# Norm weights spread by a TensorE product, small first loads on ScalarE's queue, the second token half projected first, and norms by power, VectorE and transposes

## The chip, the cores and the metric

The kernel runs on one core of a Trainium2 chip. The metric is the device time of one launch in microseconds (us), lower is better. The kernel before has a median of 930.0 us in three runs (924.01 to 930.1 us).

## What is computed

One layer of a hybrid encoder over 528 tokens (16 learned ones and 512 of the input) of width 1024, everything in float32. A root-mean-square norm gives `u`; one wide projection of `u` gives the inputs of a latent attention branch (16 heads) and of a state-space branch (SSD, four groups of eight heads, two directions); both branches are gated, projected, added to the input, and normed once more.

```python
def rmsnorm(x, w):
    y = x * lax.rsqrt(jnp.mean(x * x, axis=-1, keepdims=True) + NORM_EPS)
    return y * w

u = rmsnorm(h, norm_w)                    # h: 528 x 1024
proj = u @ w_in                           # 1024 x 8928
q_lat, kv_lat, k_rope, g_attn, z, xbc, dt_raw, merge = jnp.split(proj, offsets, axis=-1)
y_a = mla_branch(q_lat, kv_lat, k_rope, ...)            # norms q_lat and kv_lat first
y_a = (y_a * jax.nn.silu(g_attn)) @ w_attn_proj
y_s = ssd_branch(z, xbc, dt_raw, ...)                   # conv over tokens, scan, norm per group
y_s = y_s @ w_ssd_proj
gates = jax.nn.sigmoid(merge)
h = h + (gates[0] * y_a + gates[1] * y_s) @ w_out
h = rmsnorm(h, final_norm_w)
```

Seven norms lie in the way: that of `h` at the start, one for each SSD group, one for `q_lat`, one for `kv_lat` (and the last one, which the change leaves alone).

## The kernel before

Everything that feeds a product is held transposed, features on partitions and tokens along the row. A float32 product is made from three products of a reduced type: each factor is split into a high part (rounded, by ScalarE) and a low part (the rest, by VectorE), and `proj` (line 522) adds high by high, high by low and low by high, in that order. With 1024 input features these are 3 times 8 matmuls of a 128-column weight tile on 512 tokens, or on two token halves of 264 (270 where a convolution follows). The weights `wr` come by DMA in pieces of 512 KB (two buffers), are split to `wh` and `wl` (three buffers each), and are used up by TensorE.

**The start.** The token blocks `xt` (four of 128 tokens, and 16 learned ones) and the norm weights `nw` (copied to all 128 partitions by the DMA itself, two halves of 512) are loaded on SyncE's queue in the order of `LOADS` (line 44). For each block `u_stats` (564) sums the squares on ScalarE and raises the mean to the power -1/2 on GpSimd (`rr`); `u_scale` (574) multiplies by `rr` and `nw` on VectorE (`xw`); `u_split` (583) transposes on TensorE (`tr`, against the identity `ident` in the tile `cst`, itself a DMA from `masks`), and splits into `uh` and `ul`. The blocks go in the order of `UORDER`. Then come `dt_stage` (655), the projection for the time steps and the rope key, and the six projections with convolutions of group 0 (`in_units`, 768; the tiles `B`, `C`, `x`), and after them the four gates `z`.

**The norms inside.** `rms_rows` (981) squares the tiles (`sq`), adds them on VectorE, sums over partitions by a product with ones (`ssq`), takes mean and epsilon on VectorE, the power on GpSimd (`rc`), and spreads the row over all partitions by a float32 product with the identity (`rb`, line 1008). VectorE then multiplies by `rb`.

**Attention.** For each head: scores (`sc`), the maximum on VectorE, the exponential on ScalarE (`p`), transposes of the probabilities (`pt`), their split (`pT`), the product with the values (`o`, `y`). GpSimd multiplies `y` by the gate (line 1275, `YG`) and the query's rope part by the sine (line 1117, `RPE`): 8 and 4 instructions.

**What sets the order.** All code is recorded first (`_Recorder`, 94; `drive`, 1451, picks which unit of work goes on), with an estimated cost for each instruction (`_Eng`, 266; `_Queue`, 338). `order` (166) then places the instructions one after another by these costs, and that fixes each engine's instruction order. On the chip each engine runs its own list in order and waits where an operand is missing. Because one line emits every instruction, all rows carry line 263 and are told apart by their tiles.

Of the kernel before, what the change touches and what calls it, by code (L numbers as in the profile page):

```python
# [16 lines left out]
P = 128  # L17
D = 1024
NM = 16
# [22 lines left out]
NRM, YG, YL, RPE, PEL = "VVVA", "G", "V", "VGV", "V"  # L42
UORDER = (0, 1, 2, 4, 3)
LOADS = "0a1bi243"
UPOOL = ()
# [48 lines left out]
class _Recorder:  # L94
# [71 lines left out]
    def order(self):  # L166
# [41 lines left out]
        while len(out) < len(ops):  # L208
# [20 lines left out]
            if o.eng == "PE" and o.four != four:  # L229
                four, more = o.four, self.SWITCH  # L230
            elif o.both:
                lock = t + o.occ
            elif o.eng == "POOL":
                port = t + o.occ - 50.0
# [31 lines left out]
class _Eng:  # L266
# [3 lines left out]
    def __getattr__(self, op):  # L270
        fn = getattr(self.eng, op)

        def call(*args, **kw):
# [31 lines left out]
            if self.name == "PE":  # L305
                if op == "transpose":
                    occ, lat = 109.0, 271.0
                elif lhs.dtype == F32R:
                    occ = max(109.0, {270: 126.0, 264: 122.0, 256: 118.0}.get(n, 0.4476 * n + 3))
                    lat = occ + 165  # L310
                    if lhs.shape[0] == 64:
                        occ, lat = 427.0, 493.0
                else:
                    occ = max(109.0, 2 * 0.838 * n)
                    occ = occ if n > 1 else 223.0
                    occ = occ / 2 if cols == 64 else occ
                    lat = occ + 165
            elif self.name == "ACT":
                occ = (50 if psum else 99) + 0.834 * k + 95 * ptr + (60 if "accum_out" in kw else 0)
# [18 lines left out]
class _Queue:  # L338
    def __init__(self, plan, rec, eng):
        self.plan, self.rec, self.eng = plan, rec, eng  # L340

    def dma_start(self, out, in_, after=0.0):
        n = 4 * out.shape[0]
        for d in out.shape[1:]:
            n *= d
        self.plan.op("DMA", 2000.0 + n / 330.0, out, [in_], after)
        wide = "cum_rows" in in_.name
        self.rec.add("SP", self.eng.dma_start, (out, in_), {}, 420.0, (1.3 if wide else 1.1) * n / 262.0, [out], [in_],
                     extra=1000.0 if wide else 0.0)
# [3 lines left out]
def hybrid_block_kernel(ctx, tc, a, out):  # L353
# [70 lines left out]
    S = _Queue(plan, rec, nc.sync)  # L424
# [97 lines left out]
    def proj(w, src, cols, M=P, tag="m", width=HALF):  # L522
# [6 lines left out]
        seq = [(hi, 0, k) for k in range(n)] + [(hi, 1, k) for k in range(n)] + [(lo, 0, k) for k in range(n)]  # L529
        for h, s in enumerate(parts):  # L530
            o = ps[:M, :cols.stop - cols.start] if tag == "m" else ps[:M, h, :width]
            for i, (x, y, k) in enumerate(seq):
                mm(o, x[:, k, :], src[k][y][:, s], start=(i == 0), stop=(i == len(seq) - 1))
                mid[0] = h < len(parts) - 1 or i < len(seq) - 1
# [29 lines left out]
    def u_stats(c):  # L564
# [5 lines left out]
        for j in range(2):  # L570
            if (c, j) in UPOOL:
                tt(G, xw[c][j], xt[c][:, j * 512:(j + 1) * 512], nw[j], ALU.mult)

    def u_scale(c):
        R = rows(c)
        for j in range(2):
            if (c, j) in UPOOL:
                A.activation(xw[c][j], xw[c][j], AF.Copy, scale=rr[c][:, 0:1])
            else:
                V.scalar_tensor_tensor(xw[c][j][:R], xt[c][:R, j * 512:(j + 1) * 512], rr[c][:R, 0:1], nw[j][:R],  # L580
                                       op0=ALU.mult, op1=ALU.mult)
# [10 lines left out]

    steps = UORDER
    for i in range(len(steps) + 2):
        if i < len(steps):
            u_stats(steps[i])
        if 1 <= i <= len(steps):
            u_scale(steps[i - 1])
        if i >= 2:
            u_split(steps[i - 2])  # L600
# [380 lines left out]
    def rms_rows(tiles, n, dim):  # L981
        blocks = [(j, min(P, n - j)) for j in range(0, n, P)]
        acc = None
        for t in tiles:
# [5 lines left out]
            else:  # L990
                tt(V, acc, acc, q, ALU.add)
# [15 lines left out]
        for i, (j, R) in enumerate(blocks):  # L1007
            mm(pb[:, j:j + R], rc[:R, i:i + 1].broadcast_to([R, P]), ident[:R, :R])
# [474 lines left out]

    main(setup)
    fill([mark(dt_stage, "dt")])
    in_fill(0)
    for g in range(NG):
# [11 lines left out]
        fill(z_units(g))  # L1499
# [78 lines left out]
```

## Time and profile before

| | us |
|---|---|
| median of three runs | 930.0 |
| the profiled execution, its own time | 927.54 |
| its span, first to last instruction | 925.8 |
| TensorE busy in it | 880.9 |
| VectorE busy | 702.2 |
| ScalarE busy | 545.5 |
| GpSimd busy | 38.7 |

In the profile PE is TensorE, PEld its weight loads, DVE is VectorE, ACT ScalarE, POOL GpSimd, SP SyncE (SPq its queue). A row of the timeline has start, duration, engine, operation, tiles and, in brackets, how long the engine sat idle before it and what ended that. The granted clock of TensorE is 1.0 for 2.4 GHz and 0.5 for 1.2 GHz.

### The profile page before, as it was taken

How to read it: one execution, taken by the hardware profiler on the slowest of the kernel's cores; microseconds unless marked ns; L12 is line 12 of the kernel's file. 1: busy time of each engine (PE TensorE's matmuls, PEld its weight loads, DVE VectorE, ACT ScalarE, POOL GpSimd, SP SyncE). 2: the span in 40 equal slices, each digit the busy share in tenths (PEclk: the TensorE clock that was granted, in tenths of full speed). 3: DMA queues.
4: the chain of work that ended last, by engine and by line, in shares of the span. 5: the costliest groups of instructions: out<-in, count | busy, mean ns of one | idle time of the engine just before them, and what ended most of it. 6: DMA issues, size and time to landing. Idle time of an engine off the chain costs nothing.

```text
span 925.8 us, 13360 instructions
## 1 busy us (share of the span) xinstructions
PE 880.9 (95%) x5005; PEld 728.5 (79%) x5005; DVE 702.2 (76%) x1233; ACT 545.5 (59%) x1152; POOL 38.7 (4%) x32
## 2 busy tenths in 40 slices
PE   4999999999999999999999999999999999999997
PEld 4997878776899768866787788887778777888875
DVE  6797699978699599987857855979989897334364
ACT  5379468866656366875334455767777785432232
POOL 1000000100000000010002000101000000000000
PEclk8999999999999999999999999999999999999999
DMA  6474227325432333542221342212111011442222
GB/s 194 114 188 114 69 69 204 92 77 139 125 97 89 90 86 105 130 136 70 64 74 46 103 114 70 61 33 49 38 41 40 10 29 46 137 137 91 91 69 91
DMA packets 127237, 83.83 MB, mean 91 GB/s; under 512 B 26384, under 2 KB 114101, under 8 KB 127173
## 3 DMA queue, kind: packets, MB, share of 16 engines
q1 hardware_dynamic: 127173, 82.99, 32.4%
q8 instruction: 39, 0.64, 0.3%
q14 instruction: 25, 0.20, 0.1%
HBM read 80.74 MB, written 2.23 MB: 90 GB/s over the span
## 4 chain that ended last, share of the span: by engine, by line
PE 71%; DVE 18%; ACT 5%; issue 2%; POOL 2%; DMA 1%; SPq 0%; POOLq 0%; ACTq 0%; DVEq 0%
PE pj L263 50%; PE wo L263 4%; DVE x L263 4%; PE sc L263 3%; PE st L263 2%; PE yo L263 2%; PE o L263 2%; PE pt L263 2%; DVE wl L263 2%; PE tr L263 2%; DVE w L263 1%; POOL rc L263 1%; PE yd L263 1%; DVE mx L263 1%; DVE pT L263 1%
## 5 line engine op out<-in xcount | busy, mean ns | idle before, releaser
L263 DVE TENSOR_TENSOR wl<-wr,wh 128x1024 fp32r<-128x1024 f32 (+1 forms) x102 | 124.8, 1224 | 77.9 <-ACT wh L263 58.0
L263 PE MATMUL pj<-uh,wh 128*128 128x270 f32 (+3 forms) x776 | 160.6, 347 | 7.0 <-DVE yo L263 4.2
L263 ACT CAST wh<-wr 128x1024 fp32r<-128x1024 f32 (+1 forms) x102 | 106.3, 1045 | 101.3 <-PE pj L263 71.7
L263 PE MATMUL pj<-ul,wh 128*128 128x270 f32 (+3 forms) x776 | 156.1, 338 | 0.0
L263 PE MATMUL pj<-uh,wl 128*128 128x270 f32 (+3 forms) x776 | 149.8, 335 | 0.0
L263 PEld LDWEIGHTS pj<-uh,wh 128*128 128x128 f32 (+1 forms) x776 | 121.4, 190 | 28.2 <-DVE yo L263 5.7
L263 PEld LDWEIGHTS pj<-uh,wl 128*128 128x128 f32 (+1 forms) x776 | 122.4, 189 | 15.0
L263 PEld LDWEIGHTS pj<-ul,wh 128*128 128x128 f32 (+1 forms) x776 | 121.1, 189 | 13.2 <-issue 0.3
L263 ACT ACTIVATE ar<-ar,nacs 128x128 f32<-128x128 f32 x256 | 80.9, 392 | 12.9 <-DMA ar<-cum_rows 8.7
L263 PE MATMUL sc<-kst,qst 96*128 96x264 f32 (+1 forms) x384 | 66.6, 299 | 3.2 <-ACT p L263 1.7
L263 PEld LDWEIGHTS sc<-kst,qst 96*128 96x128 f32 (+1 forms) x384 | 53.4, 189 | 7.7 <-ACT p L263 3.5
L263 PE MATMUL pt<-cst,p 128*128 128x128 f32 (+1 forms) x320 | 52.1, 273 | 6.1 <-DVE pT L263 5.3
L263 ACT ACTIVATE p<-sc,mx 128x528 f32<-128x528 f32 x64 | 45.0, 704 | 19.7 <-DVE mx L263 18.1
L263 DVE TENSOR_TENSOR pT<-pt,pT 128x512 fp32r<-128x512 f32 x64 | 43.6, 684 | 12.5 <-ACT pT L263 12.3
L263 PEld LDWEIGHTS pt<-cst,p 128*128 128x128 f32 (+1 forms) x320 | 37.4, 130 | 16.9 <-DVE pT L263 4.7
L263 ACT CAST pT<-pt 128x512 fp32r<-128x512 f32 x64 | 37.1, 585 | 21.2 <-PE pt L263 20.8
L263 DVE SCALAR_TENSOR_TENSOR x<-pj,chv,x 128x528 f32<-128x528 f32 x64 | 48.6, 762 | 0.8 <-ACT x L263 0.6
L263 DVE TENSOR_REDUCE mx<-sc 128x1 f32<-128x528 f32 x64 | 44.5, 696 | 4.5 <-PE sc L263 4.3
L263 PE MATMUL o<-pT,v 128*128 128x512 f32 x128 | 46.6, 417 | 1.4 <-ACT pT L263 1.2
L263 ACT ACTIVATE w<-cbm,dt_t 128x128 f32<-128x128 f32 x128 | 40.3, 392 | 4.8 <-DVE cbm L263 4.8
L263 PE MATMUL pj<-nh,wh 128*128 128x512 f32 x128 | 39.8, 435 | 1.5 <-ACT nh L263 1.5
L263 DVE SCALAR_TENSOR_TENSOR w<-cbm,dt_t,w 128x128 f32<-128x128 f32 x128 | 38.4, 348 | 0.0
(221 smaller groups left out, 1493.0 us busy)
## 6 DMA issues: line engine op xcount, KB each, us to landing
wr<-in_w_in SPq DMA_DIRECT2D x69, 512.0 KB, 3.8
ar<-cum_rows SPq DMA_DIRECT2D x32, 512.0 KB, 5.6
wr<-in_w_ssd_proj SPq DMA_DIRECT2D x16, 512.0 KB, 3.4
wr<-in_w_attn_proj SPq DMA_DIRECT2D x8, 512.0 KB, 3.5
wr<-in_w_out SPq DMA_DIRECT2D x8, 512.0 KB, 3.6
ws<-in_w_uq SPq DMA_DIRECT2D x36, 64.0 KB, 3.0
xt<-in_x SPq DMA_DIRECT2D x4, 512.0 KB, 6.4
fin<-in_x SPq DMA_DIRECT2D x4, 512.0 KB, 3.9
```

Of the source, the lines that this page charges most:

```text
L263: o.fn(*o.args, **o.kw)
```

## The change

A line of "..." stands for unchanged code, or for cost estimates of the planner that nothing below speaks of.

```diff
-NRM, YG, YL, RPE, PEL = "VVVA", "G", "V", "VGV", "V"
-UORDER = (0, 1, 2, 4, 3)
-LOADS = "0a1bi243"
-UPOOL = ()
+NRM, YG, YL, RPE, PEL = "VVVA", "V", "V", "VVV", "V"
+LOADS = "3abi2104"
...
             elif o.eng == "POOL":
-                port = t + o.occ - 50.0
+                port = t + o.occ + 60.0
...
-    S = _Queue(plan, rec, nc.sync)
+    S, Q = _Queue(plan, rec, nc.sync), _Queue(plan, rec, nc.scalar, "ACT")
...
         if step == "i":
-            S.dma_start(ident, a["masks"][:, 0, :])
+            Q.dma_start(ident, a["masks"][:, 0, :])
         elif step in "ab":
             j = "ab".index(step)
-            w = slot([P, 512], name="nw")
-            S.dma_start(w, a["norm_w"][0, j * 512:(j + 1) * 512].partition_broadcast(P))
+            w = slot([1, 512], name="nw")
+            Q.dma_start(w, a["norm_w"][:, j * 512:(j + 1) * 512])
             nw.append(w)
         else:
             c = int(step)
             t = xt[c] = big([P, D], name="xt")
             if c == NC:
-                S.dma_start(t[:NM], a["meta_tokens"])
+                Q.dma_start(t[:NM], a["meta_tokens"])
...
+    nwb = [psm([P, 512], name="nwb") for _ in range(2)]
+    for j in range(2):
+        mm(nwb[j], ones[:1, :], nw[j][:1, :])
...
-        seq = [(hi, 0, k) for k in range(n)] + [(hi, 1, k) for k in range(n)] + [(lo, 0, k) for k in range(n)]
-        for h, s in enumerate(parts):
+        seq = [(hi, 0, k) for k in range(n)] + [(lo, 0, k) for k in range(n)] + [(hi, 1, k) for k in range(n)]
+        for h, s in list(enumerate(parts))[::-1]:
...
-                V.scalar_tensor_tensor(xw[c][j][:R], xt[c][:R, j * 512:(j + 1) * 512], rr[c][:R, 0:1], nw[j][:R],
-                                       op0=ALU.mult, op1=ALU.mult)
+            V.scalar_tensor_tensor(xw[c][j][:R], xt[c][:R, j * 512:(j + 1) * 512], rr[c][:R, 0:1], nwb[j][:R],
+                                   op0=ALU.mult, op1=ALU.mult)
...
-                tt(V, acc, acc, q, ALU.add)
+                V.scalar_tensor_tensor(acc, acc, dim * EPS / P if t is tiles[1] else 0.0, q, op0=ALU.add, op1=ALU.add)
...
-                V.tensor_scalar(rc[:rows, cs], pc[:rows, cs], 1.0 / dim, EPS, op0=ALU.mult, op1=ALU.add)
+                A.copy(rc[:rows, cs], pc[:rows, cs])
                 tt(G, rc[:rows, cs], rc[:rows, cs], mhalf[:rows, cs], ALU.pow)
+                V.tensor_scalar(rc[:rows, cs], rc[:rows, cs], dim ** 0.5, None, op0=ALU.mult)
...
-            mm(pb[:, j:j + R], rc[:R, i:i + 1].broadcast_to([R, P]), ident[:R, :R])
+            T.transpose(pb[:, j:j + R], rc[:R, i:i + 1].broadcast_to([R, P]), ident[:R, :R])
...
+    for step, c in ((u_stats, 3), (u_stats, 2), (u_scale, 3), (u_stats, 1), (u_scale, 2), (u_split, 3), (u_scale, 1), (u_split, 2),
+                    (u_split, 1)):
+        step(c)
+    begin([mark(dt_stage, "dt")])
+    for step in (u_stats, u_scale, u_split):
+        step(0)
+    first = [mark(u, ("in", 0, i)) for i, u in enumerate(in_units(0))]
+    begin(first[:1])
+    for step in (u_stats, u_scale, u_split):
+        step(NC)
     main(setup)
-    fill([mark(dt_stage, "dt")])
-    in_fill(0)
+    zs = z_units(0)
+    for k in "1a2345bcd":
+        fill([first[int(k)] if k.isdigit() else zs["abcd".index(k)]], lambda: True)
```

The norm weights now arrive as one row each and are spread to 128 partitions by a product with ones into PSUM (`nwb`), which VectorE reads in place of `nw`. They, the identity and the learned tokens are issued by ScalarE. The projection of a tile in two halves begins with the second token half, which needs blocks 3, 2 and 1 only, and inside a half the low weights come before the low activations. The gates `z` of group 0 are mixed into its convolutions.

On TensorE, the first rows of the program. `tr` are transposes of `xw`, `pj` products of the projections; before:

```order
L263 MATMUL tr_119<-cst,xw_103 128x128 x4
L263 MATMUL tr_120<-cst,xw_104 128x128 x4
L263 MATMUL tr_123<-cst,xw_105 128x128 x4
L263 MATMUL tr_124<-cst,xw_106 128x128 x4
L263 MATMUL tr_127<-cst,xw_107 128x128 x4
L263 MATMUL tr_128<-cst,xw_108 128x128 x4
L263 MATMUL tr_129<-cst,xw_111 128x16 x4
L263 MATMUL tr_130<-cst,xw_112 128x16 x4
L263 MATMUL pj_157<-uh,wh_148 96x264 x4
L263 MATMUL pj_159<-uh,wh_151 128x270
```

and of the changed kernel:

```order
L261 MATMUL nwb_102<-nw_96,ones 128x512
L261 MATMUL nwb_103<-nw_97,ones 128x512
L261 MATMUL tr_133<-cst,xw_111 128x128 x4
L261 MATMUL tr_134<-cst,xw_112 128x128 x4
L261 MATMUL tr_135<-cst,xw_109 128x128 x4
L261 MATMUL tr_136<-cst,xw_110 128x128 x4
L261 MATMUL tr_137<-cst,xw_107 128x128 x4
L261 MATMUL tr_138<-cst,xw_108 128x128 x4
L261 MATMUL pj_158<-uh,wh_140 96x264 x4
L261 MATMUL pj_161<-uh,wh_147 128x270 x3
L261 MATMUL tr_144<-cst,xw_105 128x128 x4
```

Two spreading products stand first, and the transposes of the learned tokens (two groups of 16 columns) have moved behind the first projection products.

On VectorE, around the first group's norm: `rc` is the row of 1/rms, `wl`, `w` and `ar` are instructions with two SBUF operands that belong to other work. Before:

```order
L263 TENSOR_TENSOR wl_348<-wr_337,wh_347 128x1024
L263 TENSOR_SCALAR rc_341<-ssq_340 128x4
L263 TENSOR_TENSOR wl_351<-wr_342,wh_350 128x1024
L263 TENSOR_TENSOR w_241_345<-w_241_345,ar_344 128x512
L263 TENSOR_TENSOR ar_412<-ar_412 128x512
L263 TENSOR_TENSOR ar_421<-ar_421 128x512
L263 TENSOR_TENSOR ar_433<-ar_433 128x512
L263 SCALAR_TENSOR_TENSOR x_67_171<-x_67_171,chv,rb_343 128x512 x4
```

and changed:

```order
L261 TENSOR_TENSOR wl_348<-wr_340,wh_347 128x1024
L261 SCALAR_TENSOR_TENSOR w_248_352<-cbm_304,dt_t,w_248_352 128x128 x3
L261 SCALAR_TENSOR_TENSOR z_343<-z_343,pj_337 128x512
L261 TENSOR_TENSOR xw_358<-tr_353,wst 128x512
L261 SCALAR_TENSOR_TENSOR w_248_352<-cbm_304,dt_t,w_248_352 128x128
L261 TENSOR_SCALAR rc_350<-rc_350 128x4
L261 TENSOR_TENSOR ar_429<-ar_429 128x512
L261 TENSOR_TENSOR w_248_352<-w_248_352,ar_351 128x512
L261 TENSOR_TENSOR ar_442<-ar_442 128x512
L261 TENSOR_TENSOR ar_446<-ar_446 128x512
L261 SCALAR_TENSOR_TENSOR x_81_185<-x_81_185,chv,rb_357 128x512 x4
```

Before, VectorE's `rc` stood ahead of GpSimd's power, with a run of five such instructions right behind it; now `rc` is the scaling that waits for the power, and four of that run stand behind it. On TensorE 12 products of 512 columns stand between `ssq` and `rb` before, and 4 transposes and 12 such products after.

On VectorE in attention, where the gate product enters. `o` is a head's output, `z` the gate. Before:

```order
L263 TENSOR_TENSOR y_1042<-o_1069,y_1042 64x512
L263 RECIPROCAL sm_1105<-sm_1105 128x1
L263 COPY qst_815<-qpl_1081 32x512
L263 TENSOR_TENSOR pT_1104<-pt_1103,pT_1104 128x512
L263 TENSOR_TENSOR pT_1112<-pt_1111,pT_1112 128x512
```

and changed:

```order
L261 COPY qst_811<-qpl_1083 32x512
L261 TENSOR_REDUCE mx_1108<-sc_1115 128x1
L261 RECIPROCAL sm_1107<-sm_1107 128x1
L261 TENSOR_SCALAR p_1112<-p_1112,sm_1107 128x528
L261 TENSOR_TENSOR y_1044<-o_1071,y_1044 64x512
L261 TENSOR_TENSOR pT_1106<-pt_1105,pT_1106 128x512
L261 TENSOR_TENSOR y_1044<-y_1044,z_1035 128x512
L261 TENSOR_TENSOR pT_1114<-pt_1113,pT_1114 128x512
```

The gate product is VectorE's own instruction between two splits of `pT`, and the copy to `qst` has moved ahead of the sum into `y`.

## Rows read from the trace of the kernel before

**Rows 1.** The page, part 1: busy us and share of the span.
```profile
PE 880.9 (95%) x5005; PEld 728.5 (79%) x5005; DVE 702.2 (76%) x1233; ACT 545.5 (59%) x1152; POOL 38.7 (4%) x32
```

**Rows 2.** Waits of TensorE: total us, times, longest.
```profile
PE rb L263 <- POOL rc L263: 3.7, 2, 1.9
...
PE pj L263 <- DVE B L263: 1.3, 1, 1.3
```

**Rows 3.** The timeline of the start, all engines.
```profile
1.17 0.43 SPq L263 DMA_DIRECT2D nw<-in_norm_w  x1
...
3.06 0.74 SPq L263 DMA_DIRECT2D xt<-in_x  x1
...
3.98 1.06 ACT L263 ACTIVATE junk<-xt 128x1024 f32<-128x1024 f32 x1 [1.97 <-DMA xt<-in_x]
...
6.75 0.75 DVE L263 SCALAR_TENSOR_TENSOR xw<-xt,rr,nw 128x512 f32<-128x512 f32 x1 [1.44 <-DMA nw<-in_norm_w]
8.15 1.06 ACT L263 ACTIVATE junk<-xt 128x1024 f32<-128x1024 f32 x1 [3.02 <-DMA xt<-in_x]
...
9.47 0.75 DVE L263 SCALAR_TENSOR_TENSOR xw<-xt,rr,nw 128x512 f32<-128x512 f32 x1 [1.97 <-DMA nw<-in_norm_w]
...
10.96 1.42 DVE L263 SCALAR_TENSOR_TENSOR xw<-xt,rr,nw 128x512 f32<-128x512 f32 x2 [0.67 <-POOL rr L263]
...
18.60 1.86 PE L263 MATMUL pj<-uh,wh 128*96 128x264 f32 x7
```

**Rows 4.** Stretches of the start: busy us per engine, granted clock, DMA share, GB/s.
```profile
10.00:20.00 10.00, 7.34 (x38) 6.13 (x38) 9.05 (x19) 8.24 (x17) 3.02 (x4) 0.84 0.81 205
20.00:25.00 5.00, 5.00 (x30) 5.00 (x29) 4.29 (x9) 1.17 (x2) 0.00 (x0) 0.64 0.41 107
```

**Rows 5.** The chain that ended last, in order of time: start, us, one piece.
```profile
2.59 7.07 DMA cst<-in_masks
```

**Rows 6.** DMA issues: size and us from issue to landing.
```profile
dtb<-in_dt_bias SPq DMA_DIRECT2D x1, 0.2 KB, 2.3
```

**Rows 7.** Groups by shape: count, busy us, mean ns of one row, idle before.
```profile
L263 PE MATMUL st<-xw,bt 128*128 128x512 f32 x48 | 24.9, 601 | 0.0
...
L263 PE MATMUL tr<-cst,x 128*128 128x128 f32 x64 | 9.8, 276 | 0.0
...
L263 PE MATMUL rb<-cst,rc 128*128 128x128 f32 x48 | 6.9, 288 | 3.8 <-POOL rc L263 3.7
...
L263 DVE TENSOR_TENSOR x<-x,z 128x512 f32<-128x512 f32 x16 | 10.1, 685 | 0.0
...
L263 ACT COPY bm<-tr 16x128 f32<-16x128 f32 x4 | 1.0, 247 | 0.0
```

**Rows 8.** The timeline around two of the inner norms.
```profile
173.40 4.24 POOL L263 TENSOR_TENSOR rc<-rc,mhalf 128x4 f32<-128x4 f32 x1 [155.04 <-DVE rc L263]
...
173.83 2.00 PE L263 MATMUL pj<-uh,wl 128*128 128x512 f32 x8
...
174.88 1.89 DVE L263 TENSOR_TENSOR ar<-ar 128x512 f32<-128x512 f32 x3
```

**Rows 9.** GpSimd's timeline, the second group's norm.
```profile
274.60 1.01 POOL L263 TENSOR_TENSOR rc<-rc,mhalf 128x4 f32<-128x4 f32 x1 [96.95 <-DVE rc L263]
```

**Rows 10.** Attention: the timeline at one gate product, and the wait at another.
```profile
660.64 1.28 POOL L263 TENSOR_TENSOR y<-y,z 128x512 f32<-128x512 f32 x1 [14.51 <-DVE y L263]
660.73 1.48 DVE L263 CAST qst<-qpl 32x512 fp32r<-32x512 f32 x1
...
662.99 0.44 PE L263 MATMUL pt<-cst,p 128*128 128x128 f32 x2 [1.57 <-DVE pT L263]
...
721.84 0.44 PE L263 MATMUL pt<-cst,p 128*128 128x128 f32 x2 [1.55 <-DVE pT L263]
```

**Rows 11.** The copies to `qst` on VectorE: ns min/median/max, first and last start.
```profile
L263 DVE CAST qst<-qpl x13: 416/419/1482, 572.7 to 755.3; 32x512 fp32r<-32x512 f32 x13
```

**Rows 12.** One stretch of four heads, columns as in rows 4.
```profile
660.64:719.50 58.86, 54.93 (x343) 46.82 (x342) 51.51 (x107) 43.85 (x96) 3.87 (x3) 1.00 0.15 35
```

More of the change, by code (lines that the diff above doesn't have):

```diff
@@ L318, in call @@
             elif self.name == "ACT":
-                occ = (50 if psum else 99) + 0.834 * k + 95 * ptr + (60 if "accum_out" in kw else 0)
+                occ = (50 if psum else 99) + 0.834 * k + 95 * ptr + (13 if "accum_out" in kw else 0)
                 lat = occ + 97
@@ L338, with __init__ @@
 class _Queue:
-    def __init__(self, plan, rec, eng):
-        self.plan, self.rec, self.eng = plan, rec, eng
+    def __init__(self, plan, rec, eng, name="SP"):
+        self.plan, self.rec, self.eng, self.name = plan, rec, eng, name
     def dma_start(self, out, in_, after=0.0):
@@ L347, in dma_start @@
         wide = "cum_rows" in in_.name
-        self.rec.add("SP", self.eng.dma_start, (out, in_), {}, 420.0, (1.3 if wide else 1.1) * n / 262.0, [out], [in_],
-                     extra=1000.0 if wide else 0.0)
+        if self.name == "ACT":
+            self.rec.add("ACT", self.eng.dma_start, (out, in_), {}, 120.0, 2600.0, [out], [in_])
+            return
+        self.rec.add("SP", self.eng.dma_start, (out, in_), {}, 420.0, (1.3 if wide else 1.1) * n / (420.0 if "in_x" in in_.name else 262.0), [out], [in_],
+                     extra=0.0 if wide else 2500.0 if n <= 1 << 17 else 1500.0 if "w_" in in_.name else 0.0)
 @with_exitstack
@@ L533, in proj @@
                 mm(o, x[:, k, :], src[k][y][:, s], start=(i == 0), stop=(i == len(seq) - 1))
-                mid[0] = h < len(parts) - 1 or i < len(seq) - 1
+                mid[0] = h > 0 or i < len(seq) - 1
                 if i % (PART * len(parts)) == PART * len(parts) - 1 and mid[0]:
@@ L569, in u_stats @@
         tt(G, rr[c][:R], ss[c][:R, 1:2], mhalf[:R, 0:1], ALU.pow)
-        for j in range(2):
-            if (c, j) in UPOOL:
-                tt(G, xw[c][j], xt[c][:, j * 512:(j + 1) * 512], nw[j], ALU.mult)
     def u_scale(c):
@@ L576, in u_scale @@
         for j in range(2):
-            if (c, j) in UPOOL:
-                A.activation(xw[c][j], xw[c][j], AF.Copy, scale=rr[c][:, 0:1])
-            else:
-                V.scalar_tensor_tensor(xw[c][j][:R], xt[c][:R, j * 512:(j + 1) * 512], rr[c][:R, 0:1], nw[j][:R],
-                                       op0=ALU.mult, op1=ALU.mult)
+            V.scalar_tensor_tensor(xw[c][j][:R], xt[c][:R, j * 512:(j + 1) * 512], rr[c][:R, 0:1], nwb[j][:R],
+                                   op0=ALU.mult, op1=ALU.mult)
     def u_split(c):
@@ L591, in u_split @@
             lo_of(V, ul[:, 4 * j:4 * j + 4, uc], ps[:, :, :R], uh[:, 4 * j:4 * j + 4, uc])
[L593 to L600, printed above, removed]
     chv = keep([P, 200], name="chv")
@@ L1482, in proj_fill, with begin @@
         fill([mark(lambda m=m: proj_unit(g, m), ("proj", g, m)) for m in range(4)], lambda: epi_ok(g))
+    def begin(makes, n=3):
+        for mk in makes:
+            it = Item(mk)
+            for _ in range(n):
+                it.step()
+            opened.append(it)
+    for step, c in ((u_stats, 3), (u_stats, 2), (u_scale, 3), (u_stats, 1), (u_scale, 2), (u_split, 3), (u_scale, 1), (u_split, 2),
[8 more added lines that the diff above has]
+        step(NC)
     main(setup)
-    fill([mark(dt_stage, "dt")])
-    in_fill(0)
+    zs = z_units(0)
+    for k in "1a2345bcd":
+        fill([first[int(k)] if k.isdigit() else zs["abcd".index(k)]], lambda: True)
     for g in range(NG):
@@ L1498, in hybrid_block_kernel @@
         main(lambda g=g: group_epi(g), lambda g=g: has(("yd", g, 3), *[("z", g, ti) for ti in range(4)])())
-        fill(z_units(g))
+        if g:
+            fill(z_units(g))
         if g:
```

## Prediction

> **What bounds the kernel now.** I read the page's busy times first, then TensorE's waits, then the timeline of the start, of the inner norms and of attention. TensorE is busy 95% of the span and no other engine over 76% [rows 1], so time can come out in three ways only: TensorE starts its products earlier, does less, or waits less. The start is where it loses most at once: the first projection product runs at 18.60 [rows 3]. Between there and the end its waits are small and scattered. The two of interest are 3.7 us in two pieces, where the spread row `rb` waits for GpSimd's power, and 1.3 us for the tile `B` in the first convolutions [rows 2].
>
> **The start.** Before, the first block of tokens is in at 3.98, but `xw` needs the norm weights: the first half is used at 6.75 and the second at 9.47, each after an idle VectorE waiting for that load, issued at 1.17 in the first case. The third `xw` runs at 10.96 [rows 3]. From 10 to 20 us VectorE is then busy 9.05 of 10 and ScalarE 8.24 [rows 4], so this stage is a stream of work on those two, and being earlier means starting that stream earlier.
>
> The weights now are two loads of 2 KB. A tiny load took 2.3 us to land [rows 6]; the identity, 64 KB behind the big loads of the same queue, took 7.07 [rows 5]. Issued by ScalarE from about 0.7 us on, one each 0.43 us [rows 3], they land between 3.3 and 8 us. I take 4.5, nearer the tiny load, because nothing stands ahead of them in their own queue.
>
> (By the Trainium skill, page DMA: Bandwidth & Descriptors, section Issuing engines are not separate DMA queues, this part should bring little: loads from several engines run on the same 16 DMA engines and interleave, and a second issuer saves only the issuing time. The rows agree in so far as the tiny load and the identity shared one queue and differed threefold, but no run here has two queues. By the page the weights would land with the token blocks, and the sum below would be some 2 us smaller.)
>
> The spreading product is new. The nearest row is a float32 product of 512 columns: 24.9 us for 48 rows, two rows a product [rows 7], so 1.04 us at 2.4 GHz and 2.1 at 1.2. TensorE has not run before, so I take 2.1: the first half is there at 6.6 and the second at 8.7. The second `xw` then starts at 8.7 instead of 9.47 and the third at about 9.5 instead of 10.96: the stream is 0.8 to 1.5 us ahead. ScalarE's four issues cost 4 x 0.43 = 1.7 us ahead of its first square, which fit into the 1.97 us it idled before the block came; at 0.74 each, the longest issue, they would delay it by 1.0 [rows 3]. VectorE reading `nwb` from PSUM I price at nothing (0.75 us before; even 0.1 more on ten is 1.0, and that is in the lower bound).
>
> Second, what must precede the first product shrinks. The learned tokens' two groups of transposes, with two `xw` of 0.75 us and their splits, now stand behind it (order, TensorE): another 0 to 1.5 us. Together the first product comes 0.8 to 3.0 us earlier; I take 2.0, at 16.6.
>
> Third, the clock. The granted clock means 0.84 over 10 to 20 and 0.64 over 20 to 25 [rows 4]; with 0.5 as the lower level that is 3.2 + 3.6 = 6.8 us at 1.2 GHz, of which the 5 us from 18.60 on are projection work and cost half, 2.5 us. It fell after TensorE's gaps between the first transposes. The two spreading products fill some of this. Gain 0 to 2.5, I take 0.5, since gaps before the first product remain. **Start: -2.5 us** (+1.2, from 0.8 less the two 1.0 above, to -5.5, from 3.0 and 2.5).
>
> **The gates among the convolutions.** A gate needs one VectorE pass on its result where a convolution needs five, so the products have something to run on while VectorE works off `B` [rows 2]. The wait of 1.3 us may go, or turn up elsewhere: **-0.5** (-1.3 to +1.3). The order high, low weights, then low activations changes no work: 0; its risk is a rival below.
>
> **Less work in the norms.** 48 rows of `rb`, 24 products, took 6.9 us; 64 transposes of the same size took 9.8, so 24 take 3.7 [rows 7]. **-3.2 us**, on TensorE's path at six places; both counts are of the same engine and the same size, so I give it no range.
>
> **The waits in the norms.** The power took 4.24 us at 173.40 and 1.01 at 274.60 [rows 8, 9]. In the slow case VectorE ran two-operand instructions from SBUF (`ar` from 174.88 for 1.89 us) right beside it, and GpSimd ended 0.9 us after that run. (The Trainium skill, page SBUF — State Buffer, section SBUF: two separate sides, has the two engines hold one port pair in turn, each for a whole instruction; the rows agree.) Now VectorE's next but few instruction waits for the power itself (order, VectorE), so the run cannot stand beside it. The chain gets longer by ScalarE's copy, 0.25 us [rows 7], and the hops to and from it; VectorE's scaling replaces its earlier pass. 0.25 + 1.01 + 0.6, which I allow for hops and scaling, = 1.9 us, under a cover of 12 products at 2.00 us for 8 [rows 8], 3.0 us. Both waits go, -3.7; in the pair of latent norms, where fewer products stand between, I give back 0.9. While VectorE waits, `ar` and `w` are queued behind it, and ScalarE's exponentials behind them; up to 1 us at six places, covered by products that are already split. **-2.8 us** (-3.7 to +5.3: with the power at 4.24 in all six sets the chain is 5.1 us, the cover with four transposes at 0.15 is 3.6, so 1.5 us times six, less 3.7).
>
> **Attention.** GpSimd's gate product at 660.64 stretched VectorE's copy to `qst` to 1.48 us against a median of 0.42 [rows 10, 11]; the split of `pT` queued behind it came late and TensorE waited 1.57 us, and 1.55 at 721.84 [rows 10]. These 3.1 us go. In exchange VectorE does 8 + 4 instructions more at 0.685 [rows 7], 8.2 us. It is busy 51.51 of 58.86 us per four heads there [rows 12]; three more instructions there, less the 1.06 us of stretch, are 1.0 us into 7.35 idle. I charge a tenth or so of the 8.2, 1.1: **-2.0 us** (-3.1 to +5.1, if all of it lies on the path).
>
> **Sum.** 2.5 + 0.5 + 3.2 + 2.8 + 2.0 = 11.0 us. From the profiled execution's 927.54 us: **916.5 us**. That execution is 2.5 us below the median of 930.0.
>
> **Rivals.**
> *The start gives nothing.* ScalarE and VectorE are nearly full from 10 us on [rows 4] and do the same work, and the norm weights land as late as the identity did, 7 us [rows 5]. Against it: VectorE idled before both first `xw` [rows 3]. Without the start's and the gates' 3.0: 919.5 us.
> *VectorE becomes the bound in attention.* It is busy 88% of that stage [rows 12] and the whole 8.2 us fall on the path: +5.1 instead of -2.0, so 923.6 us. Against it: TensorE's waits there are on chains through both engines, and the stretched copies go away. (The Trainium skill's page Perfetto Trace Analysis, section Optimizing Scalar/DVE Operations, would offload from a saturated VectorE, this change does the reverse; the page adds that between GpSimd and VectorE it might not help, which rows 10 bear out.)
> *The power stays slow.* Two-operand instructions of VectorE still stand beside it ahead of the one that waits, +5.3 instead of -2.8: 924.6 us. Against it: the order of rows on VectorE.
> *The low weights are late*, the one on the other side. `wl` is now needed 8 products earlier, up to 2.0 us for full tiles [rows 8], in each of 101 units of weights. If VectorE is behind, each such unit waits; 20 units at 1.2 us are +24, 940 us; slower than before from about nine units on. Against it: TensorE's list of waits names no `wl` at all, and weights are split well ahead.
>
> **Chances.** The forecast 0.55 (its own range 911 to 921), the start 0.15, VectorE 0.14, the power 0.10, late weights 0.06. A change of 1%, 9.3 us, is about what a measurement of this kernel can tell from none, so faster by over 1% means below 918.3: most of the forecast, 0.47, and a part of the start's rival, 0.06, in sum 0.53. Slower by over 1% are the late weights, 0.06; the rest, 0.41, is within 1%. The range 910 to 925 leaves out the late weights, what lies below the forecast's own range, and a part of the two rivals that end near 924.
>
> **What would show it.** Right: the first projection product near 16.6 us; `xw` number two near 8.7; `rb` as transposes with no wait; `rc` on GpSimd near 1 us; no copy to `qst` over 0.6 us. Wrong: `nwb` late, `p` or `pT` waits of TensorE grown by more than 3 us, or waits on `wl`.

## The result, and the profile after

The changed kernel takes 912.8 us (median of four runs, 912.25 to 915.12) against 927.8 us before: a ratio of 0.985, 95% interval 0.981 to 0.988, so 14 us or 1.5% less. The profiled execution took 913.33 us with a span of 911.5 us, 14.3 us shorter than the span before. The forecast was 916.5 us, in a range of 910 to 925. The total came out near the forecast, but by luck: the runs below show that two of its steps were wrong by 6 to 8 us each, in opposite directions.

Page, part 1, of the changed kernel: busy us and share of the span. The rows before are [rows 1].

```profile
PE 878.5 (96%) x4984; PEld 725.7 (80%) x4984; DVE 707.9 (78%) x1245; ACT 543.2 (60%) x1159; POOL 11.7 (1%) x20
```

TensorE is busy 2.4 us less and idle 11.9 us less. Its waits in the changed kernel (total us, times, longest):

```profile
PE sc L261 <- ACT p L261: 5.4, 9, 1.4
PE pj L261 <- DVE yo L261: 3.5, 2, 2.0
PE o L261 <- ACT pT L261: 2.9, 3, 1.1
PE pj L261 <- DVE x L261: 2.8, 2, 2.1
...
PE nwb L261 <- DMA nw<-in_norm_w: 2.2, 1, 2.2
PE pj L261 <- ACT wh L261: 1.6, 1, 1.6
...
PE pt L261 <- DVE pT L261: 0.8, 3, 0.3
...
PE rb L261 <- DVE rc L261: 0.2, 1, 0.2
```

The wait for the spread row, 3.7 us in [rows 2], is 0.2, the one on `B` is gone, and no row names `wl`. The one on `wh` is new, and that on `x` has grown from 0.6 to 2.8 us. In attention `pt` waits 0.8 us for `pT` and no longer 5.3, but the scores wait 5.4 us for ScalarE's `p` (1.7 before) and `o` 2.9 us for ScalarE's `pT` (1.2 before).

The timeline of the start, which answers to [rows 3] (start, duration, engine, operation, tiles; in brackets the idle time before):

```profile
0.73 0.75 ACTq L261 DMA_DIRECT2D nw<-in_norm_w  x2
...
2.17 3.92 PE L261 MATMUL nwb<-nw,ones 1*128 1x512 f32 x4 [2.17 <-DMA nw<-in_norm_w]
...
4.43 1.06 ACT L261 ACTIVATE junk<-xt 128x1024 f32<-128x1024 f32 x1 [0.72 <-DMA xt<-in_x]
...
6.43 0.75 DVE L261 SCALAR_TENSOR_TENSOR xw<-xt,rr,nwb 128x512 f32<-128x512 f32 x1 [0.67 <-POOL rr L261]
...
7.16 1.50 DVE L261 SCALAR_TENSOR_TENSOR xw<-xt,rr,nwb 128x512 f32<-128x512 f32 x2
...
7.24 1.97 PE L261 MATMUL tr<-cst,xw 128*128 128x128 f32 x8 [1.15 <-DVE ss L261]
...
13.72 1.97 PE L261 MATMUL tr<-cst,xw 128*128 128x128 f32 x8 [1.02 <-DVE ul L261]
...
15.51 1.99 PE L261 MATMUL pj<-uh,wh 128*96 128x264 f32 x7
...
17.30 1.05 PE L261 MATMUL tr<-cst,xw 128*128 128x128 f32 x4
```

The weights are spread from 2.17 us on, the first token block is in at 4.43, and `xw` then runs without waiting for a weight. The first projection product starts at 15.51 instead of 18.60. A second load has moved too: the identity, on which the first transposes waited until 9.79 us in the kernel before, TensorE's longest wait there:

```profile
PE tr L263 <- DMA cst<-in_masks: 9.8, 1, 9.8
```

Issued by ScalarE, it is there when the first transposes start, at 7.24. TensorE ran the rows above at the lower of its two levels: eight transposes take 1.97 us (1.33 for eight at 15.41 before), seven projection products 1.99 us (eight take 1.13 later). The granted clock reads 1.00 there in the table of stretches, as it does before TensorE had done anything at all, so in the first 15 us the durations have to be read, not that column.

GpSimd's powers in the inner norms, groups 1 and 4 (before: [rows 8, 9]):

```profile
173.24 1.01 POOL L261 TENSOR_TENSOR rc<-rc,mhalf 128x4 f32<-128x4 f32 x1 [159.39 <-ACT rc L261]
...
471.18 1.01 POOL L261 TENSOR_TENSOR rc<-rc,mhalf 128x4 f32<-128x4 f32 x1 [91.27 <-ACT rc L261]
```

The four groups take 1.01 us each. The fourth group's norm now runs 10 us ahead of those of the two latents; in the kernel before it ran between them, at 489.86 us.

### The profile page after: what moved, and what is told of

It is laid out like the page before. It is cut to its first block, busy times and chain, and to the rows that moved or that the text cites. A ratio compares the mean times of both kernels' runs of the same rounds, so it can differ in the third digit from the quotient of the medians.

```text
span 911.5 us, 13243 instructions
## 1 busy us (share of the span) xinstructions
PE 878.5 (96%) x4984; PEld 725.7 (80%) x4984; DVE 707.9 (78%) x1245; ACT 543.2 (60%) x1159; POOL 11.7 (1%) x20
## 4 chain that ended last, share of the span: by engine, by line
PE 74%; DVE 17%; ACT 4%; issue 2%; DMA 1%; POOL 0%; POOLq 0%; ACTq 0%; DVEq 0%
PE pj L261 53%; PE wo L261 4%; PE sc L261 3%; PE st L261 2%; PE yo L261 2%; PE o L261 2%; DVE x L261 2%; DVE wl L261 2%; PE pt L261 2%; PE tr L261 2%; PE yd L261 1%; DVE mx L261 1%; DVE pT L261 1%; DVE yo L261 1%; DVE C L261 1%
## 5 line engine op out<-in xcount | busy, mean ns | idle before, releaser
L261 PE MATMUL pj<-uh,wh 128*128 128x512 f32 (+3 forms) x776 | 158.8, 346 | 8.0 <-DVE yo L261 3.5
L261 PE MATMUL pj<-uh,wl 128*128 128x270 f32 (+3 forms) x776 | 157.1, 339 | 0.0
L261 PE MATMUL pj<-ul,wh 128*128 128x270 f32 (+3 forms) x776 | 150.0, 335 | 0.0
L261 DVE TENSOR_TENSOR pT<-pt,pT 128x512 fp32r<-128x512 f32 x64 | 43.8, 685 | 11.5 <-ACT pT L261 11.3
```

Of the source, the lines that this page charges most:

```text
L261: o.fn(*o.args, **o.kw)
```

## The experiments

All times are medians, each with its ratio to the kernel before, run beside it (whose medians were 926.3 to 927.8 us).

| run | us | ratio to before (95%) |
|---|---|---|
| changed kernel | 912.8 | 0.985 (0.981 to 0.988) |
| 1 attention's products back on GpSimd | 913.7 | 0.986 (0.984 to 0.988) |
| 2 inner norms undone | 928.3 | 1.001 (1.000 to 1.003) |
| 3 start undone | 927.7 | 1.001 (1.000 to 1.003) |
| 4 planner's estimates undone | 914.4 | 0.986 (0.984 to 0.988) |
| 5 gates of group 0 last | 924.4 | 0.997 (0.995 to 0.998) |
| 6 order of the power undone | 929.0 | 1.002 (1.001 to 1.003) |
| 7 spreading by products again | 915.7 | 0.988 (0.985 to 0.990) |
| 8 kernel before with the new norms alone | 913.4 | 0.986 (0.983 to 0.988) |
| 9 old power, units picked as for the new | 914.2 | 0.987 (0.984 to 0.989) |
| 10 new power, units picked as for the old | 929.4 | 1.004 (1.002 to 1.006) |
| 11 kernel before, units picked as for the new | 918.4 | 0.991 (0.989 to 0.993) |
| 12 low activations before low weights | 906.0 | 0.978 (0.975 to 0.981) |

**Run 1, attention.**

```diff
-YG, RPE = "V", "VVV"
+YG, RPE = "G", "VGV"
```

> The changed kernel with the gate product and the rope's sine product given back to GpSimd; all else as changed. Theory 1 (the prediction's step): the 3.1 us of TensorE waits on pT come back against 1.1 us of VectorE work saved, so 2.0 us slower than the changed kernel, 914.8 us; a copy to qst near 1.5 us stands in the trace again and TensorE's waits on pT rise from 0.8 to over 3 us. Theory 2 (from the changed kernel's list of waits, where the wait on pT fell from 5.3 to 0.8 us but those on p and on ScalarE's pT rose from 2.9 to 8.3): the edit exchanged one wait for another and was worth nothing, so 912 to 913.5 us, with the sum of all TensorE waits in attention within 1.5 us of the changed kernel's 11.5. Theory 3 (VectorE bound): over 1.5 us faster than the changed kernel.

913.7 us. Copies to `qst` on VectorE, minimum, median and maximum in ns; first the changed kernel, then this run:

```profile
L261 DVE CAST qst<-qpl x16: 415/418/421, 508.3 to 742.5; 32x512 fp32r<-32x512 f32 x16
```

```profile
L261 DVE CAST qst<-qpl x16: 415/418/1412, 508.1 to 740.1; 32x512 fp32r<-32x512 f32 x16
```

The stretched copy is back (1412 ns) and so are waits on `pT`, 2.3 us after 0.8. But the scores wait 3.7 us for `p` instead of 5.4, and all of TensorE's waits in attention add up to 11.4 us here and 11.5 in the changed kernel. The waits speak for theory 2: one was exchanged for another. The times do not decide: 913.7 us lies between the two theories, and the difference, 0.9 us by the medians and 1.5 by the ratios, is inside the intervals.

**Runs 2 and 3, the norms undone, the start undone.** Run 2 restores the lines marked with a minus in the norms' part of the change, run 3 those of the start (loads, order of blocks and halves, gates behind the convolutions).

> The changed kernel with the inner norms as before (VectorE ahead of the power, float32 products for the spreading). Theory 1 (the prediction's steps): +3.2 us of TensorE work and +2.8 us of waits, so 918.8 us; rb busy near 6.9 us, and a power of GpSimd above 3 us with a wait of TensorE behind it at at least one of the norms. Rival A (the waits of before were an accident of that order and not of the chain): only the 3.2 us come back, 916.0 us, with no wait on rc over 0.5 us. Rival B (the planner hides more than the sum of the pieces): under 914.5 us.

> The changed kernel with the start of before: norm weights copied to 128 partitions by the load, all loads on SyncE's queue in the earlier order, blocks 0, 1, 2, 4, 3, first token half first, gates of group 0 behind its convolutions. Theory 1 (the prediction's terms, 2.5 + 0.5): 3.0 us slower than the changed kernel, 915.8 us. Theory 2 (from the two traces: the same 144 projection products are through at 38.1 against 40.8 us, and the waits on B and C, 2.2 us, are gone): 4.9 us slower, 917.7 us. In both the first projection product is back near 18.6 us and the granted clock falls below 0.9 in 10 to 25 us. Rival (the start gives nothing later on): within 1.5 us of the changed kernel.

928.3 and 927.7 us: each gives up the whole gain of 14 us, where 6 and 3 to 5 had been expected. The parts of the change do not add up. TensorE's waits with the norms undone, then GpSimd's powers, and all seven powers as minimum, median and maximum in ns:

```profile
PE pj L261 <- ACT wh L261: 3.3, 1, 3.3
...
PE pj L261 <- ACT nh L261: 2.3, 2, 1.5
...
PE rb L261 <- POOL rc L261: 1.0, 1, 1.0
```

```profile
170.84 1.05 POOL L261 TENSOR_TENSOR rc<-rc,mhalf 128x4 f32<-128x4 f32 x1 [157.30 <-DVE rc L261]
...
484.70 4.39 POOL L261 TENSOR_TENSOR rc<-rc,mhalf 128x4 f32<-128x4 f32 x4 [106.62 <-DVE rc L261]
```

```profile
L261 POOL TENSOR_TENSOR rc<-rc,mhalf x7: 547/1009/1919, 170.8 to 488.1; 128x4 f32<-128x4 f32 x6, 16x1 f32<-16x1 f32 x1
```

No power takes 4.24 us as in [rows 8]: the first group's takes 1.05, four in a row take 4.39 with 1.92 as the longest, and TensorE waits 1.0 us for them in all. Most of the time went into waits on `wh`, `nh` and others that do not name the power, between 289 and 507 us. With the start undone the one large item is the wait on `B`:

```profile
47.55 2.17 PE L262 MATMUL pj<-uh,wh 128*128 128x270 f32 x8 [6.53 <-DVE B L262]
```

It was 1.3 us in the kernel before [rows 2], with the same start but the old order of the low parts, the old norms and the planner's old estimates. The eight products behind it take 2.17 us instead of 1.17.

**Run 4, the planner's estimates.**

```diff
-                port = t + o.occ + 60.0
+                port = t + o.occ - 50.0
...
```

> The changed kernel with the planner's cost estimates of before (port held 50 us-thousandths less instead of 60 more after a GpSimd instruction, accumulating activations 60 instead of 13 ns, loads estimated as before). No instruction is added or removed, only the order changes. Theory 1 (the prediction charged nothing for it): within 1 us of the changed kernel, 912 to 914 us. Rival (part of the gain is the better estimate): 2 us or more slower, 915 us or above. The size of the difference, of either sign, also says how far a new order alone moves this kernel, which bounds what the other differences mean.

914.4 us, 1.5 us above the changed kernel with intervals that overlap. These estimates carry no part of the gain that can be told. ("50 us-thousandths" stands for 50 ns.)

**Run 5, the gates last.**

```diff
-    for k in "1a2345bcd":
+    for k in "12345abcd":
```

> The changed kernel with the four gates of group 0 behind its six convolutions again; the new start otherwise kept. Theory 1 (the prediction's term of 0.5 us): 913.3 us, with a wait on B of at most 1.3 us as in the kernel before. Theory 2 (from the run with the start undone, where TensorE waited 6.5 us for B and its clock fell after it): the gates are what TensorE runs on there, so a wait of 4 us or more on B or C between 38 and 50 us, a granted clock under 1.0 in 40 to 60 us, and 917 to 920 us. In both the first projection product stays near 15.5 us.

924.4 us, above what theory 2 gave. The end of `B`'s convolution on VectorE and ScalarE, TensorE at the wait, and the stretches around it:

```profile
37.53 0.79 ACT L261 ACTIVATE C<-pj,chv 128x528 f32<-128x528 f32 x1 [4.26 <-PE pj L261]
...
38.22 0.60 ACT L261 ACTIVATE pj<-B 128x528 f32<-128x528 f32 x1
...
43.70 0.71 DVE L261 SCALAR_TENSOR_TENSOR B<-pj,B 128x528 f32<-128x528 f32 x1
...
44.46 2.17 PE L261 MATMUL pj<-uh,wh 128*128 128x270 f32 x8 [6.98 <-DVE B L261]
```

```profile
37.00:44.00 7.00, 0.49 (x4) 0.26 (x3) 7.00 (x13) 2.77 (x4) 0.00 (x0) 0.81 0.28 75
44.00:51.00 7.00, 6.54 (x38) 6.22 (x39) 6.12 (x11) 0.45 (x2) 0.00 (x0) 0.70 0.32 78
51.00:58.00 7.00, 7.00 (x58) 6.60 (x57) 5.09 (x13) 5.58 (x14) 0.00 (x0) 1.00 0.09 19
```

ScalarE takes the first step of `C` ahead of the tanh of `B` (the row `pj<-B`), and VectorE then does four passes of `C` before the last step of `B` at 43.70, so `B`'s PSUM bank comes free late. (In the kernel before, the last step of `B` stood ahead of the passes of `C`, at 41.38.) TensorE waits 6.98 us, and the granted clock is 0.70 in the 7 us behind it: this wait cost its own length and the slow products after it. The gates give TensorE work for just this place. Run 5 also explains most of run 3: with the gates last in both, the two differ by the rest of the start alone, 924.4 against 927.7 us (spans of 925.5 and 927.8). So the start without the gates is worth 2 to 4 us, where 2.5 was forecast, and the gates' place is the rest of what run 3 gave up.

**Runs 6 and 7, the two halves of the norms' edit.** Run 6 puts VectorE's mean and epsilon ahead of the power again and keeps the transposes; run 7 the reverse:

```diff
-            T.transpose(pb[:, j:j + R], rc[:R, i:i + 1].broadcast_to([R, P]), ident[:R, :R])
+            mm(pb[:, j:j + R], rc[:R, i:i + 1].broadcast_to([R, P]), ident[:R, :R])
```

> The changed kernel with mean and epsilon on VectorE ahead of the power again (no copy by ScalarE, no scaling behind it); the transposes stay. Theory 1 (the prediction's term): 2.8 us slower, 915.6 us, with a power above 3 us and TensorE waiting for rc. Theory 2 (from the run with the norms undone, where the power stayed at 1.01 to 1.05 us): the power's length is not set by this edit, and the time stays within 1 us of the changed kernel. Theory 3: most of that run's 15 us comes from here, 920 us or more, in waits that do not name rc.

> The changed kernel with the row of 1/rms spread by float32 products with the identity instead of transposes; the power's order stays. Theory 1 (the prediction's term): 3.2 us slower, 916.0 us, rb busy 6.9 us. Theory 2 (from the run with the norms undone, where rb took 7.8 us for the same 48 rows): 4 to 5 us slower, 917 to 918 us. Theory 3 (most of that run's 15 us comes from here): 920 us or more, in waits that do not name rc, between 280 and 510 us.

Run 7 gives 915.7 us, 2.8 us more than the changed kernel, with 7.6 us of `rb` work for 3.6: nearest to theory 1, the term of 3.2 us (the times alone would not tell, as their intervals overlap). Run 6 gives 929.0 us: theory 3. The whole loss of run 2 comes with the old order of the power, though the power lasts 1.01 to 1.05 us in the first three groups and TensorE waits for it 1.0 us in all.

**Run 8, the norms alone on the kernel before.**

> The kernel before with the new inner norms alone (epsilon in the additions, copy by ScalarE, power, scaling by VectorE, transposes); the start, attention and the planner's estimates as before. Theory 1 (the prediction's terms, 3.2 + 2.8): 6.0 us faster than the kernel before, 921 us; rb busy 3.6 us and no wait on rc. Theory 2 (from the two undone runs, each of which gave up the whole gain): the parts bring little alone, 925 us or more, with new waits of TensorE in the place of those on rc.

913.4 us: the new norms alone bring what the whole change brings. So the other edits together are worth nothing on top, in this order of the low parts, and the edit of the norms is worth 14 us and not 6. Neither theory had this.

**Runs 9 to 11, the chain and the order of the units apart.** `drive` picks the next unit of work by clocks that are advanced with each recorded instruction. A longer chain in a norm makes the norm's unit ready later, and another unit is picked. In run 9 the instructions are the old ones and the clocks the new:

```diff
-                A.copy(rc[:rows, cs], pc[:rows, cs])
-                tt(G, rc[:rows, cs], rc[:rows, cs], mhalf[:rows, cs], ALU.pow)
-                V.tensor_scalar(rc[:rows, cs], rc[:rows, cs], dim ** 0.5, None, op0=ALU.mult)
+                plan.mute = True
+                V.tensor_scalar(rc[:rows, cs], pc[:rows, cs], 1.0 / dim, EPS, op0=ALU.mult, op1=ALU.add)
+                tt(G, rc[:rows, cs], rc[:rows, cs], mhalf[:rows, cs], ALU.pow)
+                plan.mute = False
+                k = cs.stop - cs.start
+                plan.op("ACT", 60 + 0.833 * k, rc[:rows, cs], [pc[:rows, cs]])
+                plan.op("POOL", 300 + 165 * k, rc[:rows, cs], [rc[:rows, cs], mhalf[:rows, cs]])
+                plan.op("DVE", 68 + 0.6 * k, rc[:rows, cs], [rc[:rows, cs]])
```

While `mute` is set, instructions don't advance the clocks. Run 10 is the reverse on the changed kernel, and run 11 does as run 9 in the kernel before.

> The changed kernel with the old order of the power (as in the run with the power undone, 929.0 us), but the planner picks its units of work as if the chain were the new one: ScalarE's copy, power, VectorE's scaling are entered in its clocks, the old two instructions are emitted. TensorE's list then agrees with the changed kernel's but for 13 rows, where the plain undoing differs in 301. Theory U (the 14 us come from the order of the units, which the longer estimated chain has moved): 912 to 916 us, a granted clock of 0.99 or more, no waits on nh and at most one on wh over 1.5 us. Theory C (they come from the chain itself): 925 to 930 us, like the run with the power undone.

> The changed kernel with its new chain of instructions untouched, but the planner picks its units of work as if the chain were the old one. TensorE's list then agrees with that of the run with the power undone but for 6 rows. Theory U (order of the units): 925 to 930 us, waits on wh, nh and v as in that run. Theory C (the chain itself): 912 to 914 us.

> The kernel before with no instruction added, removed or altered: only the planner's clocks are told that the chain of the inner norms is ScalarE's copy, power and VectorE's scaling. Theory U: the gain of the norms alone, 14 us, less the 3.3 us of TensorE work that the transposes save and about 1 us of waits on rc, so 916 to 919 us. Theory C: 925 to 929 us, no gain.

Theory U holds in all three. The first two, with the changed kernel and run 6:

| | units as for the new chain | units as for the old chain |
|---|---|---|
| new chain | 912.8 | 929.4 |
| old chain | 914.2 | 929.0 |

The chain's own instructions are worth about 1 us at most, the order of the units 15 to 17. In the kernel before, the new order alone, no instruction altered, gives 918.4 us, 8.0 less. What it changes is seen in two stretches; run 9, then run 10 (columns as in [rows 4]):

```profile
280.00:380.00 100.00, 98.85 (x605) 81.25 (x604) 87.30 (x146) 64.81 (x153) 1.01 (x1) 1.00 0.41 107
470.00:520.00 50.00, 50.00 (x248) 41.51 (x248) 40.62 (x70) 22.97 (x41) 3.99 (x4) 0.97 0.35 90
```

```profile
280.00:380.00 100.00, 93.14 (x553) 76.21 (x552) 84.74 (x142) 63.72 (x153) 0.00 (x0) 0.97 0.39 109
470.00:520.00 50.00, 45.05 (x242) 36.78 (x242) 38.86 (x71) 23.84 (x48) 4.46 (x4) 0.86 0.24 62
```

With the old units TensorE waits in the first stretch for ScalarE's `w` (1.21 us), VectorE's `yo` (2.49) and ScalarE's `wh` (3.02). In the second the norm of the fourth group falls together with both norms of the latents. GpSimd's powers, run 10, then run 9:

```profile
490.17 4.46 POOL L262 TENSOR_TENSOR rc<-rc,mhalf 128x4 f32<-128x4 f32 x4 [104.11 <-DVE z L262]
```

```profile
471.11 1.01 POOL L262 TENSOR_TENSOR rc<-rc,mhalf 128x4 f32<-128x4 f32 x1 [91.62 <-DVE rc L262]
481.60 1.01 POOL L262 TENSOR_TENSOR rc<-rc,mhalf 128x4 f32<-128x4 f32 x1 [9.48 <-DVE rc L262]
```

Four powers in one run, the fourth group's the last of them, with little other work left for TensorE around them: it waits on `rc`, `nh` and `v`, and the granted clock is 0.86 over these 50 us. With the new units the fourth group's norm stands 10 us ahead of the other two, and TensorE is busy all 50 us. In run 11 the gain is spread: TensorE's waits between 170 and 530 us add up to 3.4 us, in the kernel before to 9.8, and the wait on `rc` among them is 0.7 instead of 3.7, though the chain is the same.

**Run 12, low activations before low weights.**

```diff
-        seq = [(hi, 0, k) for k in range(n)] + [(lo, 0, k) for k in range(n)] + [(hi, 1, k) for k in range(n)]
+        seq = [(hi, 0, k) for k in range(n)] + [(hi, 1, k) for k in range(n)] + [(lo, 0, k) for k in range(n)]
```

> The changed kernel with the products of a projection in the order of before, high by high, low activations, low weights. Theory 1 (the prediction charged nothing): 912 to 914 us. Rival (low weights late, which would show as waits on wl that this edit removes): over 1.5 us faster than the changed kernel. Since no row of the changed kernel's waits names wl, the other expectation is a difference that comes from the new order of units alone, at most 2 us of either sign.

906.0 us: 6.9 us less than the changed kernel (6 by the ratios), and the shortest time of all runs. Neither expectation fits: the rival has the sign, but no wait on `wl` stood there to be removed. One place in both traces, first the changed kernel:

```profile
114.37 1.21 DVE L261 TENSOR_TENSOR wl<-wr,wh 128x1024 fp32r<-128x1024 f32 x1
...
116.77 1.28 DVE L261 TENSOR_TENSOR yo<-yo,eac 128x512 f32<-128x512 f32 x2
...
118.10 1.94 PE L261 MATMUL pj<-uh,wh 128*128 128x270 f32 x8 [1.98 <-DVE yo L261]
```

```profile
118.00:121.50 3.50, 3.40 (x16) 3.40 (x17) 3.50 (x7) 0.61 (x1) 0.00 (x0) 0.56 0.89 255
```

```profile
111.35 1.23 DVE L261 TENSOR_TENSOR wl<-wr,wh 128x1024 fp32r<-128x1024 f32 x1
...
115.04 1.27 DVE L261 TENSOR_TENSOR yo<-yo,eac 128x512 f32<-128x512 f32 x2
...
116.37 1.27 PE L261 MATMUL pj<-uh,wh 128*128 128x270 f32 x8 [0.98 <-DVE yo L261]
```

```profile
116.00:119.50 3.50, 3.13 (x25) 3.13 (x26) 3.50 (x7) 1.29 (x4) 0.00 (x0) 1.00 0.41 130
```

In the changed kernel VectorE's split `wl` stands between two passes of `C`, 2.4 us ahead of the scan's `yo`; the product behind waits 1.98 us for `yo`, and the clock then falls to half (0.56 over the stretch; eight products in 1.94 us). In run 12 `wl` is 3.7 us ahead of `yo`, the wait is 0.98 us and the clock stays. TensorE's waits between 60 and 345 us are 3.5 us in run 12 and 8.1 in the changed kernel, and in run 12 TensorE's clock falls nowhere between the start and the tail. The fall at 118 us is not a fixed price of the order, though: the same wait for `yo`, 1.98 to 2.02 us at 116 to 120 us, was followed by the lower clock in the changed kernel and in runs 1 and 7, and not in runs 2, 4, 6, 9 and 10. Run 9:

```profile
117.56 1.27 PE L262 MATMUL pj<-uh,wh 128*128 128x270 f32 x8 [1.98 <-DVE yo L262]
```

That `wl`, now due eight products earlier, is put ahead of what TensorE needs next is what these rows suggest. The units' order has also moved a little, and the two were not separated. It has moved very little where most of the time is lost: apart from the order inside a projection, some 50 of TensorE's 1770 matmuls before 306 us stand in another place, and by then 6.7 of the 8.4 us between the two traces (spans of 911.5 and 903.1) are gone.

## Why the prediction came out as it did

*The start, -2.5 us.* Right in its size: the first product came at 15.51 (forecast 16.6) and the second `xw` at 7.16 (8.7), with the weights in at 2.17 and not 4.5. The two spreads took 3.92 us where 2 x 2.1 were assumed. One cause is missing from the sum: TensorE waited until 9.79 for the identity, and its earlier arrival, which the sum does not price, let the first transposes start at 7.24. How much each load gave was not separated. The same 144 first products of the projection (time steps, `B`, `C`) have their last eight starting here, in the changed kernel and before:

```profile
37.11 1.17 PE L261 MATMUL pj<-ul,wh 128*128 128x270 f32 x8
```

```profile
39.63 1.17 PE L263 MATMUL pj<-uh,wl 128*128 128x270 f32 x8
```

That is 2.5 us, and runs 3 and 5 say the same. (The Trainium skill, page DMA: Bandwidth & Descriptors, section Issuing engines are not separate DMA queues, has loads of several engines interleave on the same 16 DMA engines; the prediction had concluded that by the page the weights would land with the blocks. They were in use at 2.17 us and the first block at 4.43, so for loads of 2 KB this conclusion did not hold.)

*The gates, -0.5 us.* Too small. The wait on `B`, 1.3 us before, is gone, and with the gates last it is 6.98 us with slow products behind it, the largest piece of the 11.6 us that run 5 takes more. The clock was priced at the start alone; that a wait inside the kernel can be followed by half-speed products was not in the sum anywhere.

*"Changes no work: 0", the order of the low parts.* This step failed. It costs 6 to 7 us (run 12). Its rival had the place right, that the low weights are needed sooner, and the wrong sign to look for: no wait on `wl`, but, as the rows of run 12 suggest, waits on what VectorE does later because of `wl`. It is also where a part of the start's lead went. GpSimd's powers of the four groups start at 173.24, 263.22, 378.91 and 471.18 us in the changed kernel, at 173.19, 267.57, 381.13 and 473.77 in run 8, with the start of before, and at 169.03, 259.91, 371.58 and 464.32 in run 12. At the first of them the changed kernel's lead over run 8 is gone and run 12 is 4.2 us ahead. The 2 to 4 us that it is ahead of run 8 at the other three are gone by the end as well (spans of 911.5 and 911.6 us), in attention and the tail, and no run shows why.

*Less work in the norms, -3.2 us.* Right: `rb` 3.6 us, and 2.8 us in run 7.

*The waits in the norms, -2.8 us.* The signs came as named, `rb` with 0.2 us of wait and the power at 1.01 us, but not because of the new chain. The long powers stand beside a VectorE instruction with two SBUF operands, as read from [rows 8], but the new chain does not keep the two apart. Run 10 has the new chain, and its third group's power ends 0.87 us after the `wl` beside it, as that of [rows 8] does after `ar`:

```profile
383.97 1.23 DVE L262 TENSOR_TENSOR wl<-wr,wh 128x1024 fp32r<-128x1024 f32 x1 [0.17 <-ACT wh L262]
...
384.07 1.99 POOL L262 TENSOR_TENSOR rc<-rc,mhalf 128x4 f32<-128x4 f32 x1 [120.12 <-ACT rc L262]
```

With the old chain the first group's power takes 1.05 us in run 2 and 1.23 in run 11, the longest of any group 1.92 (runs 2 and 6), and 4.24 in no run but the kernel before: what stands beside the power is a matter of the order that the planner makes. And the size was wrong, since the step took the units' order for given. The longer chain in the planner's clocks moves it, and that alone is 8.0 us in the kernel before (run 11), of which the waits on `rc` are 3.0.

*Attention, -2.0 us.* Not shown: 0.9 us by the medians and 1.5 by the ratios, inside the interval (run 1), and TensorE waits as long there with the edit as without it. The sign that the prediction had named for being wrong, waits on `p` or `pT` grown by more than 3 us, did occur for `p` (1.7 to 5.4), while the waits on `pT` fell by 2.4 in sum (4.5 less for `pt`, 2.1 more for `o`).

*The sum.* Step by step, from the ratios and 927 us: the order of the units -8 (run 11), the rest of the norms -5 (run 8 less run 11; 3.3 of it `rb`), start, gates, attention and estimates -7 (run 12 less run 8), the order of the low parts +6 (changed kernel less run 12): -14. The forecast had -6 for the norms instead of -13, -5 for the third step and 0 for the last. It came near by luck, because the 7 us that it did not see in the norms and the 6 to 7 that it priced at nothing almost cancelled. The steps hold in this order only: from other starting points the same edits gave other prices, as runs 3 and 5 show.

## What to carry to other kernels

Where a planner's estimates set the order, an edit acts first through the order it makes: compare the order of the units before pricing a single instruction, and hold the plan fixed (as in runs 9 and 10) to see what the edit itself is worth. A reordering that "changes no work" moves the due time of its inputs; look at what the producing engine then does later. Undo parts one at a time, also those that were priced at nothing: the best kernel here, 906.0 us, is the change without one such part.

## What the runs showed of the hardware that was not expected

A wait of TensorE of about 2 us or more inside the kernel was often, not always, followed by a stretch at the lower clock: after 1.98 us at 118.10 (0.56 over 3.5 us), after 6.98 us in run 5 (0.70 over 7 us), and not after 2.14 us at 272.24 in the changed kernel. One and the same wait of about 2 us for `yo` was followed by it in three runs of eight. (The Trainium skill, page TensorE: Matmul & The Clock Gate, section HAM oscillation — how this bites in real kernels, has gaps put TensorE back to half rate so that the next products start slow; the rows agree on what a gap can do.) Rows with the eight products of 128x270 show it without the clock column: 1.17 us at full speed, 1.94 to 2.17 in such a stretch.

Loads of 2 KB issued on ScalarE's queue at 0.73 us were in use at 2.17, while 512 KB blocks went out on SyncE's queue beside them. A queue of its own did not do as much for a larger load: the 64 KB of learned tokens, issued by ScalarE behind the two loads of 2 KB and the identity, took 5.9 us to land in the changed kernel, where the 64 KB identity behind the blocks on SyncE's queue had taken 7.07 [rows 5].

```profile
xt<-in_meta_tokens ACTq DMA_DIRECT2D x1, 64.0 KB, 5.9
```

GpSimd's power on a 128x4 tile took 1.01 us in all four groups of the changed kernel. In five traces nine of them took 1.86 to 4.24 us, and each of the nine ended 0.87 or 0.88 us after the last of VectorE's `wl`, `ar` or `nl` beside it, all of them with two operands in SBUF.
